# Four modulation groups of the first layer change their stage

## The chip, the core and the metric

The kernel runs on one core of one Trainium2 chip. The metric is the device time of one execution in microseconds (us). The program is one long stream of instructions per engine: TensorE (PE, with its weight loads listed apart as PEld), VectorE (DVE), ScalarE (ACT), GpSimd (POOL) and SyncE (SP), which issues nearly all DMA transfers. In the profile, L247 means line 247 of the kernel.

## The reference, cut to what matters

Two groups of 128 tokens (context and latent) pass through two layers with the same weights. Each layer has a mixer sub-layer and a feed-forward sub-layer, and both are steered by a modulation vector that depends on a conditioning vector only, not on the tokens:

```python
mod = silu(cond) @ w_mod[l] + b_mod[l]            # (2048) x (2048, 12288), for two conds
sh1, sc1, g1, sh2, sc2, g2 = split(mod, 6)
h = rmsnorm(x) * (1 + sc1) + sh1
x = x + g1 * rmsnorm(mixers(h) @ w_out)           # attention, Fourier, RWKV-7 scan
h = rmsnorm(x) * (1 + sc2) + sh2
x = x + g2 * rmsnorm(conv_ffn(h))                 # 2048 -> 2 x 5632 -> 2048
```

Everything is float32. The last piece of a layer's modulation, g2, is used only when the last part of the feed-forward is written out.

## The kernel before

Activations are kept transposed: channels on the 128 partitions, the 256 tokens of both groups along the free dimension. All large weights are streamed once from HBM. A weight block of 256 rows by 512 columns (512 KB) is loaded by `weights_` (L388) into one of the seven buffers of the pool `raw`, cast by ACT to float32r as `hi` (L398), and DVE writes the rest, `raw - hi`, as `lo` (L399). The matmuls then work on the pair: in the mixer's projections three passes per tile (`mm3`, L408 to L410, 256 columns each), in the feed-forward one pass of 512 columns for `hi` (L437) and one of 256 for `lo` (L438).

**Modulation.** The 12288 columns of a layer's modulation are cut into 24 groups of 512 columns: group 4*s+k is quarter k of piece s (sh1, sc1, g1, sh2, sc2, g2), so groups 20 to 23 are g2. `modulation` (L239 on) is a generator that computes one group on TensorE, in five steps. Four steps each load two blocks of 512 KB of `w_mod` (L234) and issue four float32 matmuls on them (L247; eight records in the trace, two for each matmul) into the bank `mb`. The fifth lets DVE transpose the bank (L250, tile `pm`). The closing part, four tiny matmuls (L254, tile `mc`) and one or two small DVE additions (`mod_end`, L304), comes with the call that starts the next group. After the input projection of the first layer the blocks of `w_mod` take their buffers from the same pool of seven as the weights do (`mraw`, `self.early = 0`).

**What sets their place.** A queue `modq` holds the groups that TensorE computes: 24 of layer 0, then 8 to 19 of layer 1. The other 12 of layer 1 are computed on DVE (`modulation_v`, lines L266 to L286, tiles `vraw`, `va`, `vb`) during the two feed-forwards. Each matrix product calls `tick` after each of its weight blocks, and the tick runs as many steps of the queue as a rate has accumulated:

```python
def tick(self, n=1.0):
    self.credit += self.rate * n
    while self.credit >= 1:
        self.credit -= 1
        self.mod_step()
```

`gemm` and `gemm_wide` call `self.tick(0.5)` once per 256 rows of weights. The rate is a constant per stage: `AR` in the outer input projection, `MR[l][0..6]` in the seven stages of the mixer, `QR[l]` in the fourth part of the output projection, `FR[l]` in the feed-forward:

```python
step(0, self.in_proj(l, h, st, ["kv"]))
step(1, ... in_proj ["q"] merged with attention)
step(2, ... in_proj ["xf"])
step(3, self.ticked(self.fourier(st)))
step(4, self.merge(wo(2, ev1), self.heads(l, st, (0, 1)), 16, QM[2]))
step(5, self.merge(wo(0, ev2), self.heads(l, st, (2, 3)), 16, QM[3]))
step(6, wo(1, ev2))
```

`step(n, main)` sets `self.rate = MR[l][n]` and drives the RWKV scan beside `main`. Each of these products has eight ticks of a half, that is 4.0, and the Fourier stage has two whole ones. After them come `wo(3)` with `QR`, the norm, and the feed-forward with `FR`: 11 blocks of up-projection with 16 half ticks each and 11 of down-projection with 8 each, 264 half ticks or 132 ticks. `need` runs steps at once where a group is wanted and not there yet: groups 8 to 11 ahead of `wo(3)`, 12 to 19 in the second `pre_norm`, 20 to 23 ahead of the last down-projection.

Of the kernel before, what the change touches and what calls it, by code (L numbers as in the profile page):

```python
# [33 lines left out]
for _t in (VEC, VEC2):  # L34
# [17 lines left out]
    [[0.8, 0.8, 0.578], [0.88, 0.8, 0.8], [0.96, 0.8, 0.8], [1.0], [1.0, 1.0, 1.0, 1.0], [1.287, 1.3, 1.183, 1.3], [1.45, 1.45, 1.45]],  # L52
]
MR = [
    [1.2, 1.2, 1.2, 2.3, 2.3, 2.185, 4.0],
    [2.4, 2.4, 2.4, 2.4, 2.4, 2.4, 4.5],
]
AR = [
    [2.25, 2.5, 2.5, 0.0],
    [0.0, 0.0, 0.0, 0.0],  # L60
]
QR, FR = [2.0, 1.0], [0.165, 0.4]

VG = [[(1, j) for j in (0, 4, 1, 5, 2, 6, 3, 7)], [(1, j) for j in range(20, 24)]]
VR = [0.58, 0.4]
# [1314 lines left out]
```

## Time and profile before

| | us |
|---|---|
| median of 3 runs | 2700.96 |
| lowest, highest | 2700.59, 2710.13 |
| the profiled execution, its own time | 2702.25 |
| its span in the trace | 2700.5 |

The stages of the profiled execution, by the first matmul of each, are: set-up and outer input projection to 177.3, mixer of layer 0 to 544.8, its `wo(3)` and norm to 607.8, feed-forward of layer 0 to 1396.7, then layer 1: input projection to 1503.6, mixer to 1876.2, `wo(3)` and norm to 1928.3, feed-forward to 2677.2, output to 2700.5. A stretch A:B is given in us from the span's start. Busy time is time with at least one instruction of an engine running; an instruction's record includes its passage through the engine, so consecutive matmuls overlap, and what one costs is read from start to start.

### The profile page before, as it was taken

How to read it: one execution, taken by the hardware profiler on the slowest of the kernel's cores; microseconds unless marked ns; L12 is line 12 of the kernel's file. 1: busy time of each engine (PE TensorE's matmuls, PEld its weight loads, DVE VectorE, ACT ScalarE, POOL GpSimd, SP SyncE). 2: the span in 40 equal slices, each digit the busy share in tenths (PEclk: the TensorE clock that was granted, in tenths of full speed). 3: DMA queues.
4: the chain of work that ended last, by engine and by line, in shares of the span. 5: the costliest groups of instructions: out<-in, count | busy, mean ns of one | idle time of the engine just before them, and what ended most of it. 6: DMA issues, size and time to landing. Idle time of an engine off the chain costs nothing.

```text
span 2700.5 us, 45794 instructions
## 1 busy us (share of the span) xinstructions
PE 2598.5 (96%) x18019; PEld 2141.4 (79%) x18019; DVE 1969.5 (73%) x3316; ACT 1313.4 (49%) x2065; POOL 69.1 (3%) x114
## 2 busy tenths in 40 slices
PE   7999999979999999999989999999799999999998
PEld 4578788748888888888869777778588888888886
DVE  3467857469977898869666768575899669865675
ACT  2256545246554455445434555443555545544553
POOL 1101000000000000000000000000000000000000
PEclk9999999989999999999989999999899999999998
DMA  9965646776777787777655777366377567555552
GB/s 363 382 210 197 218 145 193 253 268 208 252 240 268 250 269 241 250 251 239 204 175 149 238 254 258 125 208 202 99 260 242 188 219 257 188 187 189 186 187 86
DMA packets 316184, 593.93 MB, mean 220 GB/s; under 512 B 22726, under 2 KB 37602, under 8 KB 315968
## 3 DMA queue, kind: packets, MB, share of 16 engines
q1 hardware_dynamic: 314336, 589.54, 65.6%
q8 instruction: 141, 2.31, 0.3%
q0 software_dynamic: 1632, 1.46, 0.2%
q14 instruction: 75, 0.61, 0.1%
HBM read 583.78 MB, written 7.14 MB: 219 GB/s over the span
## 4 chain that ended last, share of the span: by engine, by line
PE 86%; DVE 6%; DMA 3%; ACT 2%; issue 1%; SPq 0%; ACTq 0%; DVEq 0%
PE wm L437 37%; PE wm L438 18%; PE mb L247 5%; PE mm L408 4%; PE mm L409 4%; PE mm L410 4%; PE b L408 2%; PE b L409 2%; PE b L410 2%; PE px L1091 1%; DMA raw<-in_w_in 1%; PE pr L1085 1%; DMA raw<-in_w_out 1%; DVE lo L399 1%; PE vb L286 1%
## 5 line engine op out<-in xcount | busy, mean ns | idle before, releaser
L398 ACT CAST hi<-raw 128x1024 fp32r<-128x1024 f32 (+1 forms) x712 | 735.0, 1033 | 890.6 <-PE wm L437 605.4
L399 DVE TENSOR_TENSOR lo<-raw,hi 128x1024 fp32r<-128x1024 f32 (+1 forms) x712 | 855.9, 1203 | 403.8 <-ACT hi L398 388.6
L437 PE MATMUL wm<-hx,hi 128*128 128x512 f32 x2816 | 990.0, 397 | 10.9 <-DVE hx L591 10.9
L438 PE MATMUL wm<-hx,lo 128*128 128x256 f32 x2816 | 785.2, 279 | 0.0
L437 PEld LDWEIGHTS wm<-hx,hi 128*128 128x128 f32 x2816 | 530.0, 188 | 145.2 <-DVE hx L591 14.3
L438 PEld LDWEIGHTS wm<-hx,lo 128*128 128x128 f32 x2816 | 532.4, 189 | 2.6 <-issue 1.7
L437 PE MATMUL wm<-g,hi 128*128 128x512 f32 x1408 | 496.0, 398 | 0.0
L438 PE MATMUL wm<-g,lo 128*128 128x256 f32 x1408 | 393.6, 280 | 0.0
L437 PEld LDWEIGHTS wm<-g,hi 128*128 128x128 f32 x1408 | 265.2, 188 | 68.7 <-issue 7.1
L438 PEld LDWEIGHTS wm<-g,lo 128*128 128x128 f32 x1408 | 266.3, 189 | 3.2 <-issue 2.9
L280 DVE SCALAR_TENSOR_TENSOR va<-vraw,cst,va 128x512 f32<-128x512 f32 x360 | 256.4, 749 | 0.9 <-DMA vraw<-in_w_mod 0.7
L247 PE MATMUL mb<-raw,cst 128*32 128x512 f32 x1152 | 198.7, 614 | 9.6 <-DVE mod L304 5.1
L408 PE MATMUL mm<-hx,hi 128*128 128x256 f32 x544 | 158.5, 295 | 5.6 <-ACT hx L590 4.1
L409 PE MATMUL mm<-hx,hi 128*128 128x256 f32 x544 | 156.2, 288 | 0.5
L410 PE MATMUL mm<-hx,lo 128*128 128x256 f32 x544 | 155.1, 287 | 0.0
L408 PE MATMUL mm<-mx,hi 128*128 128x256 f32 x512 | 152.7, 299 | 1.8 <-ACT mx L367 1.3
L409 PE MATMUL mm<-mx,hi 128*128 128x256 f32 x512 | 146.7, 287 | 0.2 <-DVE mx L368 0.2
L410 PE MATMUL mm<-mx,lo 128*128 128x256 f32 x512 | 145.2, 287 | 1.5 <-DVE lo L399 1.5
L408 PEld LDWEIGHTS mm<-hx,hi 128*128 128x128 f32 x544 | 104.0, 193 | 34.1 <-issue 16.6
L408 PEld LDWEIGHTS mm<-mx,hi 128*128 128x128 f32 x512 | 98.0, 192 | 26.9 <-issue 21.4
L409 PEld LDWEIGHTS mm<-hx,hi 128*128 128x128 f32 x544 | 104.9, 193 | 5.4 <-issue 4.0
L410 PEld LDWEIGHTS mm<-hx,lo 128*128 128x128 f32 x544 | 104.5, 193 | 4.3 <-issue 3.9
(346 smaller groups left out, 3330.2 us busy)
## 6 DMA issues: line engine op xcount, KB each, us to landing
raw<-in_ffn_w_up SPq DMA_DIRECT2D x352, 512.0 KB, 4.4
raw<-in_w_mod SPq DMA_DIRECT2D x288, 512.0 KB, 5.6
raw<-in_ffn_w_down SPq DMA_DIRECT2D x176, 512.0 KB, 4.3
vraw<-in_w_mod SPq DMA_DIRECT2D x96, 512.0 KB, 5.0
raw<-in_w_in SPq DMA_DIRECT2D x80, 512.0 KB, 5.6
raw<-in_w_out SPq DMA_DIRECT2D x64, 512.0 KB, 5.2
raw<-in_w_uq SPq DMA_DIRECT2D x16, 384.0 KB, 4.0
raw<-in_w_in SPq DMA_DIRECT2D x16, 320.0 KB, 4.2
```

The lines of the kernel that those rows point to most:

```text
L247: nc.tensor.matmul(b[32 * q:32 * q + 32, :], self.cst[:, 4 * kg + q, :], r[:, f, :], start=kg == 0, stop=kg == 3)
L280: nc.vector.scalar_tensor_tensor(a, r[:, f, :], c, a, op0=ALU.mult, op1=ALU.add)
L286: nc.tensor.matmul(b2[:, a, g:g + 1], acc[g][:, 128 * a:128 * a + 128], self.c(C_ONE, 1), start=a == 0 and g == 0, stop=a == 3 and g == 1)
L398: nc.scalar.copy(hi[:, :, 0:w], r)
L399: nc.vector.tensor_tensor(lo[:, :, 0:w], r, hi[:, :, 0:w], op=ALU.subtract)
L408: mm(out, whi, xhi, start=start, stop=False)
L409: mm(out, whi, xlo, start=False, stop=False)
L410: mm(out, wlo, xhi, start=False, stop=stop)
L437: mm(ps[m], hi[:, kk, s], x[:, :, kk, :], start=ki == 0 and k2 == 0 and kk == 0, stop=False)
L438: mm(ps[m][:, 0, :], lo[:, kk, s], x[:, 0, kk, :], start=False, stop=ki == n - 1 and k2 == 1 and kk == 1)
L1085: mm(pr[js, n, :], AP[n // 4, d][ks, n % 4, js], rh[ks, n, :], start=n == 0, stop=n == 7, tile_position=(0, 32 * j))
L1091: mm(px[js, n, :], XT[js, 8 * d + n, :], R[js, n, :], start=n == 0, stop=n == 7, tile_position=(32 * j, 32 * j))
```

## The change

Only rates of layer 0 change: those of the mixer's first three stages and of the two merged output projections go up, and that of the feed-forward goes down. The sequence of steps in the queue and the work of each step stay as they are.

```diff
 MR = [
-    [1.2, 1.2, 1.2, 2.3, 2.3, 2.185, 4.0],
+    [2.2, 2.2, 2.2, 2.3, 3.1, 3.1, 4.0],
     [2.4, 2.4, 2.4, 2.4, 2.4, 2.4, 4.5],
 ]
 AR = [
     [2.25, 2.5, 2.5, 0.0],
     [0.0, 0.0, 0.0, 0.0],
 ]
-QR, FR = [2.0, 1.0], [0.165, 0.4]
+QR, FR = [2.0, 1.0], [0.02, 0.4]
```

## Rows read from the trace of the kernel before

**Rows 1.** The page: span, and part 1, busy us and share.
```profile
span 2700.5 us, 45794 instructions
...
PE 2598.5 (96%) x18019; PEld 2141.4 (79%) x18019; DVE 1969.5 (73%) x3316; ACT 1313.4 (49%) x2065; POOL 69.1 (3%) x114
```

**Rows 2.** Stretches: mixer, feed-forward, each of layers 0 and 1; all engines.
```profile
core 0: us, PE busy (x) PEld busy (x) DVE busy (x) ACT busy (x) POOL busy (x), PEclk, DMA share, GB/s
177.30:544.80 367.50, 357.06 (x3333) 285.64 (x3331) 250.12 (x514) 182.71 (x368) 26.23 (x38) 0.99 0.63 208
...
607.80:1396.70 788.90, 787.20 (x4542) 667.93 (x4543) 652.23 (x978) 391.68 (x526) 0.00 (x0) 0.99 0.72 240
...
1503.60:1876.20 372.60, 357.50 (x3370) 285.19 (x3369) 255.31 (x519) 186.77 (x372) 24.92 (x38) 1.00 0.65 219
...
1928.30:2677.20 748.90, 747.28 (x4310) 650.55 (x4311) 566.35 (x834) 389.78 (x524) 0.00 (x0) 1.00 0.61 199
```

**Rows 3.** The same stretches, line L247 alone: PE busy, PEld busy, clock, DMA.
```profile
177.30:544.80 367.50, 53.45 (x336) 9.01 (x336) 0.99 0.63 208
...
607.80:1396.70 788.90, 18.11 (x136) 2.67 (x136) 0.99 0.72 240
1503.60:1876.20 372.60, 55.65 (x360) 9.77 (x360) 1.00 0.65 219
```

**Rows 4.** The same, line L254 alone: layer 0's mixer and feed-forward.
```profile
177.30:544.80 367.50, 2.71 (x80) 1.71 (x80) 0.99 0.63 208
...
607.80:1396.70 788.90, 0.99 (x32) 0.63 (x32) 0.99 0.72 240
```

**Rows 5.** Timeline of PE around one step in the feed-forward: start, us, what.
```profile
644.75 0.27 PE L438 MATMUL wm<-hx,lo 128*128 128x256 f32 x1
...
648.57 0.28 PE L438 MATMUL wm<-hx,lo 128*128 128x256 f32 x1
648.78 1.07 PE L247 MATMUL mb<-raw,cst 128*32 128x512 f32 x8
649.77 0.50 PE L437 MATMUL wm<-hx,hi 128*128 128x512 f32 x1
...
650.23 0.40 PE L437 MATMUL wm<-hx,hi 128*128 128x512 f32 x1
...
654.83 0.40 PE L437 MATMUL wm<-hx,hi 128*128 128x512 f32 x1
```

**Rows 6.** Timeline of PE around one step in the mixer of layer 0.
```profile
238.84 0.28 PE L410 MATMUL mm<-hx,lo 128*128 128x256 f32 x1
239.05 1.06 PE L247 MATMUL mb<-raw,cst 128*32 128x512 f32 x8
240.05 0.39 PE L408 MATMUL mm<-hx,hi 128*128 128x256 f32 x1
```

**Rows 7.** Groups by line, feed-forward of layer 0, then of layer 1: L286.
```profile
L286 PE MATMUL vb<-const,va 128*128 128x1 f32 x128 | 15.5, 252 | 0.0
...
L286 PE MATMUL vb<-const,va 128*128 128x1 f32 x64 | 7.4, 245 | 0.0
```

**Rows 8.** Two short stretches of layer 0, columns as in the first stretches.
```profile
492.80:499.70 6.90, 6.90 (x40) 4.02 (x37) 0.00 (x0) 1.42 (x3) 0.00 (x0) 0.51 0.69 245
1318.90:1325.70 6.80, 6.80 (x26) 6.03 (x26) 2.87 (x6) 0.31 (x1) 0.00 (x0) 0.50 0.26 84
```

**Rows 9.** Waits in 177.3:544.8: who for whom, total us, times, longest.
```profile
ACT hi L398 <- DMA raw<-in_w_out: 22.0, 5, 7.1
```

**Rows 10.** Waits of SP's queue, 177.3:544.8.
```profile
SPq L234 <- PE mb L247: 89.0, 22, 17.4
SPq L388 <- PE mb L247: 57.6, 18, 7.7
```

**Rows 11.** Waits of SP's queue, 607.8:1396.7.
```profile
SPq L388 <- PE mb L247: 21.7, 16, 3.0
```

**Rows 12.** The page, part 6: loads of `w_mod` for TensorE.
```profile
raw<-in_w_mod SPq DMA_DIRECT2D x288, 512.0 KB, 5.6
```

**Rows 13.** Line L250: shortest, median, longest ns, first and last start.
```profile
L250 DVE STREAM_TRANSPOSE pm<-mb x36: 674/711/719, 25.5 to 1856.1; 128x512 f32<-128x512 f32 x36
```

## The prediction

> **What bounds the kernel now.** I read the page's head first: PE is busy 96% of the span, VectorE 73% [rows 1]. A mean over stages does not say what a step is worth, so I cut the span at the first matmul of each stage and compared the two layers [rows 2]. In the feed-forward of layer 0 PE is busy 787.2 of 788.9 us: it never waits, and anything taken off it there comes off the time. In layer 0's mixer it is busy 357.1 of 367.5 us, so at most 10.4 us are idle: it is nearly the bound there too. Work is therefore moved from one stretch in which TensorE is full to another in which it is almost full, and the question is what one step costs in each.
>
> **How many steps move.** Layer 0's mixer adds up, stage by stage, 3 x 4 x 1.2 + 2 x 2.3 + 4 x 2.3 + 4 x 2.185 + 4 x 4.0 = 52.9 steps; after the change 3 x 4 x 2.2 + 2 x 2.3 + 8 x 3.1 + 4 x 4.0 = 71.8. With the fractions carried along this is 52 steps before and 71 after. The feed-forward's 132 ticks give 22 steps at 0.165 and 3 at 0.02. So 19 steps move: 15 matmul steps, the four transposes of groups 20 to 23, and three of the four closings (that of group 23 comes with the next step, in the feed-forward). What is left of the feed-forward's steps is the beginning of layer 1's group 8, as now; layer 1 starts from the same state of the queue, and nothing in it changes. Groups 12 to 19, which the second norm needs, are ready earlier; groups 20 to 23 are needed much later, so no `need` is forced.
>
> **What the feed-forward gives back.** The rows show 136 records of L247 there, that is 17 steps [rows 3]; one more ran in the gap ahead of it. In the timeline a `lo` matmul starts at 648.57 and the next `hi` at 649.77 with one step between [rows 5]: 1.20 us, where without a step it is 0.11 to 0.12, so a step costs 1.09 us. (17 x 1.09 = 18.5, against 18.1 us of busy time.) Three steps stay, so 14 go: 15.3 us. A closing is 0.99 / 4 = 0.25 us [rows 4]; three make 0.8. The fifteenth step ran in the norm's gap, where PE waits for the norm anyway; I give it 0.5 between nothing and 1.09.
>
> There is a second item, seen only between the rows. From 644.75 to 648.57 there are 11 pairs of `hi` and `lo`, 347 ns each; from 650.23 to 654.83, after the step, 13 pairs of 354 ns [rows 5]. How often the stream is in the slower pace I take from the layers: the feed-forward of layer 0 is 788.9 - 748.9 = 40.0 us longer than layer 1's [rows 2], with the same matmuls. 18.5 us are steps, 1.0 closings, 15.5 - 7.4 = 8.1 the closings of the groups on VectorE [rows 7], 3.4 half of a 6.8 us stretch in which the granted clock was 0.50, 1.2 instead of 2.4 GHz [rows 8]. That leaves 9.0 us, which the slower pace would explain, since 2112 pairs by 7 ns are 14.8 us. With three steps instead of seventeen some of it comes back, between nothing (one early step sets the slow pace and it stays) and all 9.0. The three stand at half ticks 20, 120 and 220 of 264, so most of the stream still lies behind a step; I take 2.5. Sum: 15.3 + 0.8 + 0.5 + 2.5 = 19.1 us less, bounds 16.1 and 26.2.
>
> **What the mixer pays.** In a dense stretch a step costs the same: 238.84 to 240.05 less 0.12, that is 1.09 us [rows 6]. Over the whole stage it is more, because steps are split by other work when the second of their two loads is late: 53.45 / 42 = 1.27 us in layer 0 (two of them at half clock, [rows 8]), 55.65 / 45 = 1.24 in layer 1 [rows 3]. I take 1.24: 15 x 1.24 = 18.6, and three closings of 2.71 / 10 = 0.27 [rows 4], 0.8, in all 19.4. The floor is what the idle time could swallow: 19.4 - 10.4 = 9.0. The ceiling comes from the layers: layer 1's mixer has 45 steps and lasts 372.6 us, layer 0's 42 and 367.5 [rows 2, 3]; 5.1 / 3 = 1.7 us per step gives 26.3. Some waits will be covered by the added work (I take 2 us) and some weights will come later (2 us, see the rival), so 19.4 stands.
>
> **What travels along.** Thirty loads of 512 KB, 15.7 MB [rows 12], enter SP's queue in the mixer. It moves 208 GB/s x 367.5 us = 76 MB now; 92 MB in some 387 us are 238 GB/s, which the feed-forward moves today at 240 without PE idling [rows 2]. So bandwidth hides them; if it did not, 15.7 MB at 240 GB/s would be 65 us, which no row suggests. The four transposes are 4 x 0.71 = 2.8 us of VectorE [rows 13] in a stage where it is busy 250 of 367 us; in the feed-forward it was no bound at 652 of 789. Both I cost at nothing. If VectorE were the cover that is gone in the scan, it would cost the 2.8 us at most.
>
> A rule of the Trainium skill bears here: its page Perfetto Trace Analysis, section Identifying the Most-Contended Engine, says that matmul busy time is a poor measure of TensorE's headroom and that the busy share of weight loads is the better one. By that share the mixer has more room (285.6 / 367.5 = 78%) than the feed-forward (667.9 / 788.9 = 85%), and if the added work took that room first, the mixer would grow by its floor, 9.0 us, and the time would fall by about 10. The layers' comparison above does not bear this out: three steps more, 5.1 us more.
>
> **Sum.** 2702.25 - 19.1 + 19.4 = 2702.6 us for the profiled execution. It stands 1.3 us above the median of the runs, so 2701 us for the median.
>
> **The rivals.** *The mixer swallows the steps.* In layer 0's mixer the scan makes PE wait for VectorE and ScalarE; steps placed in these waits are free. With all 10.4 us used and the feed-forward wholly in the faster pace, 9.0 - 26.2 = -17.2: 2684 us. For it: TensorE's idle time is there, and its steps are independent of the scan. Against it: TensorE takes its instructions in order, and a tick does not know where a wait will be; layer 1's mixer, with more steps in the early stages, still has 15.1 us idle [rows 2]. It decides if the mixer grows by less than about 5 us.
>
> *The seven buffers.* A block of `w_mod` holds a buffer from its load until its step. In the mixer weight loads already wait 57.6 us in 18 waits for such a buffer, 3.2 each and up to 7.7 [rows 10], in the feed-forward 21.7 us in 16, 1.4 each [rows 11]. ScalarE then waited five times for a block of the output projection, 22.0 us, up to 7.1 [rows 9]. Today PE has other work in most of these waits. With rates of 3.1 in the two merged projections two such waits in the open would cost 14.2 us, and a stretch at half clock behind them 3.4 [rows 8]: 2701 + 17.6 = 2719 us. For it: the feed-forward has long matrix products as a cover and the mixer has not. Against it: layer 1's mixer takes 2.4 everywhere and idles no more than 5 us longer. Three uncovered waits of the mean length, or two long ones, decide it. The Trainium skill (Perfetto Trace Analysis, section Optimization Strategy) says that gaps that repeat on the engine that should be full can mean too few buffers; no row shows PE waiting so today.
>
> *The change moves less than it says.* A rate could round away, or `need` could pull steps back. The count above excludes it; the time would be that of before, 2701, and no outcome could be told from the forecast's.
>
> **How the numbers follow.** A difference of 0.5%, 13.5 us, is about what a measurement of this kernel can tell from no change. I give the forecast, an exchange at nearly the same price, 0.80, the third rival included, the swallowing mixer 0.08, the buffers 0.12. The bounds of the two sums give 9.0 - 26.2 = -17 to 26.3 - 16.1 = +10, and a first uncovered wait with half a clock stretch would add some 3 to the top: 2684 to 2715. Cutting the lower tail, where two unlikely ends must meet, leaves 2688 to 2714 with less than 2 in 10 outside. Faster by over 0.5% 0.08, within 0.80, slower 0.12.
>
> **What the profile after would show.** Step count: 24 records of L247 in layer 0's feed-forward instead of 136, and some 456 instead of 336 in the mixer. The feed-forward of layer 0 at about 770 us, the mixer at about 387. If the feed-forward shrinks by 26 the pace was the larger item; if the mixer grows by less than 9 it had room that the idle time does not show; if it grows by over 30, look for ScalarE waiting on loads of the output projection, PE idle above 15 us and more stretches at half clock. Layer 1 should keep its 1280 us to within 3; if it moves, the prediction is wrong in a place that it left out.

## The result, and the profile after

The changed kernel takes 2722.39 us (median of 5 runs, 2718.52 to 2725.47), the kernel before beside it 2704.48 us (5 runs): 1.0063 times as long, 95% interval 1.0046 to 1.0080, that is 12 to 22 us more. The forecast was an exchange at 2701 us with a range of 2688 to 2714 us, so it was wrong: the change is slower, by more than the noise of the runs. Of the 21 us between 2722 and 2701, 18 are the change; the rest is the kernel before itself, whose median was 2700.96 in the three runs that the forecast started from. The profiled execution took 2725.47 us.

The head of the page after, to be held against [rows 1]:

```profile
span 2723.7 us, 45803 instructions
...
PE 2612.1 (96%) x18019; PEld 2151.1 (79%) x18019; DVE 1971.0 (72%) x3316; ACT 1314.4 (48%) x2065; POOL 68.0 (2%) x114
```

The work is the same, and TensorE is busy 13.6 us longer with it in this profile. The heads of the other profiles below read 2598.6 and 2610.2 us before, 2599.3, 2609.5 and 2605.0 after, so most of these 13.6 belong to the one execution. What differs in all of them is TensorE's idle time: 102 to 103 us of the span before, 112 to 116 after. The stretches, cut as in [rows 2], with the gap of the second norm between the first layer's mixer and its feed-forward:

```profile
175.30:575.60 400.30, 385.90 (x3483) 295.37 (x3483) 254.26 (x525) 182.50 (x367) 25.01 (x38) 0.98 0.68 229
575.60:642.50 66.90, 47.55 (x349) 30.88 (x347) 43.00 (x74) 26.16 (x42) 1.30 (x2) 0.86 0.68 236
642.50:1406.90 764.40, 762.72 (x4399) 660.92 (x4400) 647.70 (x966) 392.44 (x526) 0.00 (x0) 1.00 0.69 228
...
1513.90:1898.20 384.30, 366.99 (x3371) 290.99 (x3370) 256.09 (x519) 186.06 (x372) 25.08 (x38) 0.97 0.63 213
...
1949.80:2701.30 751.50, 749.75 (x4310) 651.52 (x4311) 567.41 (x834) 389.46 (x524) 0.00 (x0) 1.00 0.61 198
```

The feed-forward of layer 0 gave back 788.9 - 764.4 = 24.5 us, more than the forecast's 19.1. Its mixer grew from 367.5 to 400.3 us, by 32.8 where 19.4 was said. The gap grew from 63.0 us (544.8 to 607.8 before) to 66.9, and layer 1's mixer, which the change does not name, from 372.6 to 384.3 us. Line L247 by the same stretches, beside [rows 3]:

```profile
175.30:575.60 400.30, 73.36 (x456) 12.52 (x456) 0.98 0.68 229
...
642.50:1406.90 764.40, 3.19 (x24) 0.47 (x24) 1.00 0.69 228
```

456 records in the mixer and 24 in the feed-forward: the steps moved exactly as counted.

**Taking the clock out.** Single profiles of one and the same program differ in how long the granted clock was 0.50. So I multiply each span by its mean granted clock: the length at full speed, as far as TensorE sets the length (a stretch where it does not is shown under *whole_setup*). In three profiles of the kernel before it is 2649.2, 2650.1 and 2650.8 us, in four of the changed kernel 2663.8, 2662.1, 2665.5 and 2664.0 us (spans and clocks in the table behind the experiments). The change costs some 14 us at full speed. By stretch, each length less half of its time at 0.50 (the trace gives these times; a row prints the clock only in hundredths):

| us at full speed | before, 3 profiles | after, 4 profiles | mean difference | forecast |
|---|---|---|---|---|
| mixer, layer 0 | 364.0 to 364.6 | 391.8 to 395.0 | +29.0 | +19.4 |
| gap of its second norm | 55.0 to 56.3 | 57.3 to 57.5 | +1.6 | -0.5 |
| feed-forward, layer 0 | 783.2 to 783.7 | 761.8 to 762.6 | -21.4 | -18.6 |
| layer 1, end to end | 1256.6 to 1257.9 | 1259.0 to 1264.1 | +4.4 | 0 |

The sum is +13.6. Ten of it are what the mixer took above its forecast.

**The rival that looked likelier than the others, the seven buffers, is a small part at most.** The waits of SP's queue and of ScalarE in the mixer after:

```profile
SPq L234 <- PE mb L247: 112.5, 36, 22.7
...
SPq L388 <- PE mb L247: 33.7, 20, 4.1
```

```profile
ACT hi L398 <- DMA raw<-in_w_in: 21.6, 7, 9.7
ACT hi L398 <- DMA raw<-in_w_out: 21.4, 7, 9.6
```

and, of the same waits before, the one that neither [rows 9] nor [rows 10] has:

```profile
ACT hi L398 <- DMA raw<-in_w_in: 1.9, 1, 1.9
```

Weight loads wait less for a block's buffer than before (33.7 us against 57.6, [rows 10]), and ScalarE waits for the output projection as long as before (21.4 against 22.0, [rows 9]). One wait did grow: ScalarE's for blocks of the input projections, from 1.9 to 21.6 us (10.7 to 19.8 in the other three profiles after). Little of it reaches TensorE: the recorded waits of its projection matmuls for a cast block (L408 and L410) add up to 1.1 us before and 2.4 after, those of their weight loads to 1.5 and 5.9. The larger item stands in TensorE's own order. The timeline of PE at the beginning of the mixer after:

```profile
177.30 0.28 PE L410 MATMUL mm<-hx,lo 128*128 128x256 f32 x1
177.50 1.04 PE L247 MATMUL mb<-raw,cst 128*32 128x512 f32 x2
178.48 1.12 PE L840 MATMUL b<-sq,const 128*128 128x512 f32 x2
179.44 0.60 PE L853 MATMUL b<-const,v 128*128 128x128 f32 x4
179.97 1.06 PE L247 MATMUL mb<-raw,cst 128*32 128x512 f32 x6
180.96 0.39 PE L408 MATMUL mm<-hx,hi 128*128 128x256 f32 x1
```

A step is four matmuls, 8 records. Here one of the four runs alone, 177.50 to 178.48, and after a piece of the scan the other three, 179.97 to 180.96. Each piece takes 0.98 or 0.99 us; a whole step takes 1.00 us from its start to the next instruction ([rows 6]). The four write four strips of 32 partitions and run side by side; a part of them costs as much as all four. I cut all of L247 in the first mixer into such pieces (runs of records with no other matmul between; time from the first one's start to the next other matmul's, half-clock pieces left out of the means):

| records in a piece | before, second profile: pieces, us each | after, second profile |
|---|---|---|
| 1 to 3 | 9: five of 0.98 to 1.00 us, four of 0.05 (another matmul starts beside them) | 10, of 0.98 to 1.98 us, mean 1.08 (with waits) |
| 4 | 3, 0.98 | 4, 0.98 |
| 5 to 7 | 9, 0.95 to 1.62 | 8, mean 1.21 (with waits) |
| 8 | 20, 1.00 | 19, 1.00 |
| 10 to 16 | 6, 1.84 or 1.85 | 15, 1.84 to 1.87 |
| all pieces, time at full speed | 47, 48.6 us | 56, 71.2 us |

So 15 more steps take 22.6 us, 1.51 each. The rest of the mixer's growth is in other lines, among them the projections (tile `mm`: 152.6 to 153.0 us in the profiles before, 154.3 to 157.2 after, by the same count). By stages, at full speed, the mixer's first three, which take ten of the 15 steps, grew by 18.4 us, its last three by 10.6.

### The profile page after: what moved, and what is told of

The parts are those of the page before. It is cut to its first block, busy times and chain, and to the rows that moved or that the text cites. A ratio compares the mean times of both kernels' runs of the same rounds, so it can differ in the third digit from the quotient of the medians.

```text
span 2723.7 us, 45803 instructions
## 1 busy us (share of the span) xinstructions
PE 2612.1 (96%) x18019; PEld 2151.1 (79%) x18019; DVE 1971.0 (72%) x3316; ACT 1314.4 (48%) x2065; POOL 68.0 (2%) x114
## 5 line engine op out<-in xcount | busy, mean ns | idle before, releaser
L437 PEld LDWEIGHTS wm<-hx,hi 128*128 128x128 f32 x2816 | 530.0, 188 | 140.7 <-DVE hx L591 13.8
L438 PE MATMUL wm<-g,lo 128*128 128x256 f32 x1408 | 391.8, 279 | 0.0
L247 PE MATMUL mb<-raw,cst 128*32 128x512 f32 x1152 | 202.0, 609 | 6.6 <-DMA raw<-in_w_mod 3.8
L408 PE MATMUL mm<-hx,hi 128*128 128x256 f32 x544 | 160.1, 298 | 5.5 <-ACT hx L590 4.1
L410 PE MATMUL mm<-hx,lo 128*128 128x256 f32 x544 | 156.0, 289 | 1.8 <-DVE lo L399 1.8
L408 PE MATMUL mm<-mx,hi 128*128 128x256 f32 x512 | 152.2, 299 | 1.2 <-ACT mx L367 1.1
L410 PE MATMUL mm<-mx,lo 128*128 128x256 f32 x512 | 146.0, 288 | 3.6 <-DVE lo L399 3.5
L408 PEld LDWEIGHTS mm<-hx,hi 128*128 128x128 f32 x544 | 105.3, 195 | 34.6 <-issue 15.0
L408 PEld LDWEIGHTS mm<-mx,hi 128*128 128x128 f32 x512 | 97.7, 191 | 30.6 <-issue 25.8
L410 PEld LDWEIGHTS mm<-hx,lo 128*128 128x128 f32 x544 | 105.9, 195 | 7.4 <-issue 5.1
```

Of the source, the lines that this page charges most:

```text
L247: nc.tensor.matmul(b[32 * q:32 * q + 32, :], self.cst[:, 4 * kg + q, :], r[:, f, :], start=kg == 0, stop=kg == 3)
L408: mm(out, whi, xhi, start=start, stop=False)
L410: mm(out, wlo, xhi, start=False, stop=stop)
L437: mm(ps[m], hi[:, kk, s], x[:, :, kk, :], start=ki == 0 and k2 == 0 and kk == 0, stop=False)
L438: mm(ps[m][:, 0, :], lo[:, kk, s], x[:, 0, kk, :], start=False, stop=ki == n - 1 and k2 == 1 and kk == 1)
```

## Experiments

Theories: *splits* (steps laid among the scan and the projections are taken apart, and each part costs a whole one), *loads and buffers* (15.7 MB more arrive in the mixer), *place* (one of the rates is to blame), *order* (the build arranges layer 1 anew, although its rates are the same), *chance* (the loss belongs to one execution). *Price* in the expectations is a moved step that costs some 2 us in the mixer, for whatever reason. Times are medians; each ratio is to the kernel before, on the same chip.

**The changed kernel once more** (no edit).

> The changed kernel once more, nothing altered. Three theories of its 0.6%. Price: a modulation step costs about 2 us in the first layer's mixer instead of 1.24; order: the instructions of the second layer stand in another order, although its rates did not change, and that costs some 14 us there; chance: the second layer's 14 us (1280.5 to 1294.4 us from the end of the first feed-forward to the end of the second) were this one execution's, with 17 us at half clock in its mixer where the kernel before had none. Price and order: 18 to 23 us above the kernel before, second layer again at 1292 to 1296 us. Chance: the second layer within 3 us of 1280 in this profile, and 5 to 12 us above the kernel before.

2725.6 us, 1.0072 (1.0053 to 1.0091). The loss stands. Its profile shows layer 1's mixer at 376.8 us instead of 384.3, with the granted clock at 1.00 instead of 0.97:

```profile
1512.90:1889.70 376.80, 359.49 (x3369) 286.07 (x3369) 256.12 (x519) 186.28 (x372) 25.04 (x38) 1.00 0.65 217
```

So most of what the first profile showed in layer 1 was the clock of that execution.

**Only the early stages' rates, and only the merged projections'.**

```
early:  MR[0] = [2.2, 2.2, 2.2, 2.3, 2.3, 2.185, 4.0]   FR[0] = 0.072
late:   MR[0] = [1.2, 1.2, 1.2, 2.3, 3.1, 3.1, 4.0]     FR[0] = 0.11
```

> Only the first three rates go up (2.2), and the feed-forward keeps 10 of its 22 steps: 12 steps move into the projections kv, q and xf, none into the merged output projections. The instructions of the second layer stand in the order of the changed kernel. Price with the projections as the place: first layer's mixer 20 us or more above its 367.5 us, feed-forward about 12 us below 788.9. Order: second layer 1292 to 1296 us, as in the changed kernel, and 15 us or more above the kernel before in all. Chance: second layer near 1280 us, 3 to 8 us above the kernel before.

> Only the two merged output projections go to 3.1, and the feed-forward keeps 15 steps: 7 steps move. The order in the second layer is a third one. Price with the output projections as the place (buffers held, weights late): mixer 15 us or more above 367.5 us. Price with the projections as the place: mixer plus 7 to 10 us, feed-forward minus 8, no difference in all from the first layer. Order: the second layer anywhere between 1275 and 1296 us, and the time follows it.

Early: 2725.49 us, 1.0077 (1.0060 to 1.0093). Late: 2715.68 us, 1.0046 (1.0029 to 1.0063). L247 in their mixers, early first:

```profile
175.80:574.40 398.60, 65.92 (x408) 10.79 (x408) 0.97 0.65 215
```

```profile
177.30:558.60 381.30, 56.38 (x376) 9.37 (x376) 0.99 0.65 215
```

At full speed the mixer is 388.3 us with 51 steps and 376.2 with 47: +24 for 9 and +12 for 5, no cheaper per step than all 15 together. No single rate is to blame. By the count of the table above, only 4.8 of the 12 us in *late* are L247's own, and 12.4 of the 24 in *early*; the rest stands in the projections (3.5 and 8.2) and other lines. Splits alone explain neither run.

**Nothing moved, one neutral number changed.**

```
-QR, FR = [2.0, 1.0], [0.165, 0.4]      (the kernel before)
+QR, FR = [2.0, 1.0], [0.16, 0.4]
```

> The kernel before with a feed-forward rate of 0.16 instead of 0.165: no step changes its stage, 22 steps stay in the feed-forward, some one or two ticks later. The first layer's mixer is instruction for instruction that of before; the second layer's order changes in 74 places on TensorE. Price: first layer as before within 3 us, no change in all (within 4 us). Order: the second layer moves by 5 us or more one way or the other and the time with it. Chance: differences only in half-clock stretches that another profile would not repeat.

2711.94 us, 1.0027 (1.0016 to 1.0039): 7 us for a number that moves no step out of its stage. TensorE's order in the first mixer is that of before, and that stretch is 364.3 us at full speed, as before; in layer 1 the order differs in some 70 places. There the time went:

```profile
1504.20:1887.70 383.50, 364.33 (x3371) 289.29 (x3370) 255.75 (x519) 185.71 (x372) 28.24 (x38) 0.98 0.64 213
```

1264.0 us for layer 1 at full speed, against 1256.6 to 1257.9. The changed kernel has some 40 such places there. That nothing in layer 1 changes was true of the source, not of the program built from it. Six profiles with the changed kernel's order there give 1258 to 1267 us, four with that of before 1257 to 1259: some 4 us, with ends that touch.

**The last moved groups without their loads.** Groups 20 to 23 of layer 0 multiply a tile that is already on the chip; their blocks of `w_mod` are not loaded.

```
-                r = self.mod_raw(w, i, 512 * kg + 256 * e)
+                r = (self.later.rearrange("p (c n) -> p c n", c=2) if l == 0 and i >= 20
+                     else self.mod_raw(w, i, 512 * kg + 256 * e))
```

> The changed kernel without the loads of the four moved groups: groups 20 to 23 of layer 0 multiply a tile that is resident anyway, so their 30 loads in the mixer and 2 beyond it are left out and g2 of layer 0 is wrong; every TensorE, VectorE and ScalarE instruction stays. So far the first layer's mixer is 392 to 395 us long with half-clock time taken out at half, against 364 before, 1.9 us per moved matmul step. Theory loads (the moved blocks hold buffers and make the weights late): the mixer falls to about 383, the 19 us of TensorE time alone, and the kernel by 8 to 12 us against the changed one. Theory place (what costs is that steps on TensorE stand between the scan's and the products' instructions, with or without loads): the mixer stays at 390 or above and the time within 4 us of the changed kernel.

2714.16 us, 1.0049 (1.0031 to 1.0066). Mixer and gap:

```profile
179.40:573.80 394.40, 379.58 (x3484) 291.68 (x3482) 257.07 (x529) 185.06 (x369) 24.95 (x38) 0.99 0.64 213
573.80:634.20 60.40, 47.12 (x351) 30.12 (x347) 39.95 (x71) 24.04 (x40) 1.30 (x2) 0.84 0.36 112
```

The run tests less than its expectation says. The steps without loads are the last ten of the mixer and six in the gap behind it (529.2 to 606.9 us), and 20 loads are missing in the mixer, 12 in the gap. The rates of the first three stages draw earlier groups forward, and these keep their loads. The mixer is still 391.0 us at full speed, so the volume of the last groups' loads is not its price; whether the earlier loads in the first stages cost something is not shown. The steps are still split (11 pieces of 2 records, 9 of 6), nearly all of them steps with loads; of those without, two are. What the run gains is in the gap: 51.0 us at full speed instead of 57.4, with 112 GB/s there instead of 236.

**One more buffer for the blocks** (`RAW` 7 to 8; for want of room `VRAW` 3 to 2).

> The changed kernel with eight buffers instead of seven for weights and modulation blocks, and two instead of three for VectorE's own modulation blocks to make room. Theory loads by buffers held: the mixer of layer 0 at 385 us or less (half-clock time taken out at half) instead of 392 to 395. Theory place: 390 to 396. The second layer's order changes too, so only the first layer's stages are read.

2723.49 us, 1.0078 (1.0066 to 1.0090). Not faster. The mixer was 387.5 us at full speed, between the two forecasts, with 6 pieces of 2 records instead of 10; of the 5.8 us less than in the changed kernel 4.6 are L247's own, which leaves little for the buffers. The feed-forward took 3.5 us more.

**The other direction**: steps of layer 1's groups from its mixer into layer 0's feed-forward.

```
-    [2.4, 2.4, 2.4, 2.4, 2.4, 2.4, 4.5],        (MR[1] of the kernel before)
+    [1.6, 1.6, 1.6, 1.6, 1.6, 1.6, 4.5],
-QR, FR = [2.0, 1.0], [0.165, 0.4]
+QR, FR = [2.0, 1.0], [0.3, 0.4]
```

> The opposite direction: the first layer's rates as before, but 18 more steps (groups 8 to 11 of layer 1) come into its feed-forward (rate 0.3), out of the second layer's mixer, whose rates fall to 1.6. If a step costs 1.09 to 1.5 us in the feed-forward and 1.5 to 2 in a mixer: first feed-forward at 788.9 + 15 x 1.1 to 1.5 = 805 to 812 us, second mixer 371 - 15 x 1.5 to 2 = 341 to 349 us with half-clock time taken out, in all 0 to 13 us faster than the kernel before. If the price is the same in both, no change; if the order of the second layer decides, anything within 8 us.

2709.56 us, 1.0029 (1.0014 to 1.0044): slower, where 0 to 13 us less was expected.

```profile
604.40:1410.10 805.70, 804.00 (x4679) 669.61 (x4680) 656.86 (x990) 391.72 (x526) 0.00 (x0) 1.00 0.77 252
1517.00:1883.80 366.80, 349.85 (x3226) 286.51 (x3225) 251.28 (x507) 186.88 (x372) 23.95 (x38) 0.98 0.55 182
```

At full speed the feed-forward pays 18 us, and layer 1's mixer, with 14 steps fewer (248 records instead of 360), gives back 11, that is 0.8 each. A mixer step is worth 0.8 us where it is taken from 45 in layer 1 and costs 1.9 where it is added to 42 in layer 0, so the price is no constant. How it depends on the count is not shown: layer 1's order is rebuilt here too, which alone was worth 7 us in *shift*.

**A second profile of the kernel before** (no edit).

> The kernel before once more, for a second profile of it. Both theories: first mixer 367 us again within 4 us, second layer from 1277 to 1290 us. Theory chance: its half-clock stretches in the two mixers differ by several us from the 6.8 and 3.4 us of the first profile. Theory order: the second mixer, with half-clock time taken out at half, again at 371 us within 1 us.

2703.23 us, span 2701.4, mixers of 364.6 and 380.5 us. Layer 1's mixer was 372.6 in the first profile; at full speed it is 371.0 there and 372.0 here.

**Whole steps.** Both loads first, then the four matmuls, those of the later load ahead, so that the build can lay all four side by side. Put into the changed kernel (*whole*) and into the kernel before (*whole_before*):

```
-            for e in range(2):
-                r = self.mod_raw(w, i, 512 * kg + 256 * e)
-                for f in range(2):
-                    q = 2 * e + f
-                    nc.tensor.matmul(b[32 * q:32 * q + 32, :], self.cst[:, 4 * kg + q, :], r[:, f, :], ...)
+            r = []
+            for e in range(2):
+                r.append(self.mod_raw(w, i, 512 * kg + 256 * e))
+            for q in (2, 3, 1, 0):
+                nc.tensor.matmul(b[32 * q:32 * q + 32, :], self.cst[:, 4 * kg + q, :], r[q // 2][:, q % 2, :], ...)
```

> The changed kernel, with one difference: both loads of a modulation step are issued first and then its four matmuls, the two that need the later load ahead, so that the four stand side by side in TensorE's order. Theory, splitting: a piece of one to four matmuls takes about 1.0 us, because the four fill four 32-column groups of the array together, so the mixer's 57 steps cost 71.5 us in 56 pieces where whole they would cost some 56 to 58. Then layer 0's mixer without its half-clock loss falls from 392 to 395 us to 377 to 382, its L247 pieces of 2 and 6 records are gone, and the run is 2706 to 2714 us. Rival, waiting: TensorE then stands waiting for the later of the two loads, and the mixer stays at 388 us or more although the pieces are whole, with PE waits on DMA at L247 of 8 us or more; time 2720 to 2730 us.

> The kernel before with the same difference as in the run above and no other. Splitting: layer 0's 42 mixer steps cost 48.6 us in 47 pieces; whole they cost about 42, so the mixer falls from 364 to 357 to 360 us and the time by 0 to 10 us. The pair then tells the price of a moved step without splits: mixer of the run above less mixer of this one, over 15, should be 1.1 to 1.4 us, as forecast, instead of 1.9. Rival, waiting: the difference stays at 1.8 us or more per step, so that the price lies in the place and not in the splits.

Whole: 2703.27 us, 0.9993 (0.9979 to 1.0006). Whole_before: 2694.74 us, 0.9962 (0.9944 to 0.9980). The first mixer is 382.9 and 363.6 us at full speed: 19.3 us for the 15 steps and three closings, the forecast's 19.4. By the medians the change still costs 8.5 us with whole steps in both kernels, so the splits are about half of its 18. *Whole* came out below its forecast of 2706 to 2714 us, for it gains ahead of the mixer too, and its mixer just above its 377 to 382. No piece shorter than 8 records is left in that mixer (32 of 8, 11 of 16, one of 24). L247 ahead of the mixer and in it, first in *whole*, then in *whole_before*:

```profile
0.00:160.20 160.20, 39.05 (x264) 5.92 (x264) 0.93 1.00 361
160.20:551.60 391.40, 58.04 (x456) 10.31 (x456) 0.98 0.70 234
```

```profile
0.00:160.10 160.10, 38.01 (x264) 5.71 (x264) 0.94 1.00 360
160.10:528.80 368.70, 44.23 (x336) 7.99 (x336) 0.99 0.64 206
```

(58.04 - 44.23) / 15 = 0.92 us per added step; a step is 58.04 / 57 = 1.02 and 44.23 / 42 = 1.05 us in the mean, where it was 1.27 to 1.29. So the 19.4 came out partly by chance: the steps' own busy time is 13.8 us of it, not 18.6, and the rest is waiting and other lines. And the kernel before got nothing for whole steps in its own mixer, 363.6 us against 364.0 to 364.6:

```profile
160.10:528.80 368.70, 351.78 (x3331) 287.61 (x3330) 247.63 (x513) 181.94 (x367) 26.45 (x38) 0.99 0.64 206
```

TensorE's busy time there fell from 357.06 to 351.78 us, and its idle time rose from 10.4 to 16.9. With 42 steps, what whole steps save came back as idle time; with 57, most of it came off the length (next experiment). What *whole_before* gains lies ahead of the mixer, where the modulation's first groups were split as well.

**Which part of it does what.** *whole_later* is the changed kernel with whole steps from the first mixer on (setup as it was); *whole_setup* the kernel before with whole steps in setup alone.

```
+            r, last = [], not self.early        (whole_setup: self.early)
...
+            for q in (2, 3, 1, 0) if last else range(4):
```

> The changed kernel with the four matmuls of a step kept together from layer 0's mixer on, and its setup as it was. If the extra price of the moved steps is the splitting, layer 0's mixer without its half-clock loss is 380 to 385 us as in the run with whole steps everywhere (383.0), not 392 to 395, the stretch ahead of the mixer stays at 175 to 177 us, and the time is 2709 to 2718 us, some 10 below the changed kernel. If the mixer was shorter there only because more of its work had been done ahead of it, the mixer is back at 390 us or more and the time at 2722 to 2728 us.

> The kernel before with the four matmuls of a step kept together ahead of layer 0's mixer alone; TensorE's order in the feed-forward of layer 0 and in the whole of layer 1 is that of before, and most of the first mixer's. If the gain of the kernel before with whole steps everywhere (2694.7 us) lies in the stretch ahead of the mixer, that stretch is about 160 us instead of 177 here too and the time is 2688 to 2696 us. If that stretch only gets ahead on work that the mixer then lacks, the mixer grows by as much and the time stays at 2701 to 2706 us.

Whole_later: 2715.03 us, 1.0044 (1.0026 to 1.0061), by the ratios 5 to 8 us below the changed kernel (1.0063 and 1.0072), with intervals that overlap; the mixer tells more. All engines in it, L247 in it, and the same place as in the timeline above:

```profile
178.20:569.90 391.70, 372.23 (x3484) 292.74 (x3483) 253.66 (x526) 182.25 (x367) 25.22 (x38) 0.98 0.70 233
```

```profile
178.20:569.90 391.70, 58.83 (x456) 10.30 (x456) 0.98 0.70 233
```

```profile
180.22 0.28 PE L410 MATMUL mm<-hx,lo 128*128 128x256 f32 x1
180.43 1.06 PE L247 MATMUL mb<-raw,cst 128*32 128x512 f32 x8
181.43 1.13 PE L840 MATMUL b<-sq,const 128*128 128x512 f32 x2
```

The mixer is 383.2 us at full speed, and 382.0 in the second profile below: some 10 less than the changed kernel's 391.8 to 395.0. Of these, 3 lie in the first three stages and 7 in the last three; the ten steps added to the first three cost 15 us even whole. The step that took 177.50 to 178.48 and 179.97 to 180.96 takes 180.43 to 181.43. Whole_setup: 2694.5 us, 0.9964 (0.9953 to 0.9976), with layer 1 in the order of before. Its stretch ahead of the mixer is 161.4 us, and L247 costs 40.24 us there for 264 records, against 60.98 before:

```profile
0.00:161.40 161.40, 40.24 (x264) 6.05 (x264) 0.92 0.99 357
```

```profile
0.00:177.30 177.30, 60.98 (x264) 8.91 (x264) 0.99 0.91 326
```

The second line is the kernel before. That is the whole gain of *whole_before*, and this version is faster than the kernel before and the changed one.

In this stretch the product of length and clock misleads. Four steps of setup, first in *whole_setup* wholly at 0.50, then in the second profile of the kernel before (there partly in halves) at 1.00:

```profile
27.80:40.00 12.20, 7.74 (x32) 0.83 (x32) 2.81 (x3) 1.04 (x1) 0.00 (x0) 0.50 1.05 387
```

```profile
26.50:38.40 11.90, 7.93 (x32) 1.15 (x32) 3.83 (x5) 1.33 (x2) 0.00 (x0) 1.00 1.05 386
```

TensorE waits for blocks of `w_mod` in both, and at half the clock they took 0.3 us more, not twice as long. The products of the three versions with whole steps in setup are therefore too low as lengths at full speed; for these the spans and times count.

**Is the rest the clock?** Unchanged kernels, one profile each: before, after twice, whole_later.

> The kernel before, unchanged, for a third profile. If the time at half clock belongs to the program, its mean granted clock is 0.981 again and the span 2700 to 2702 us; if it belongs to the execution, the clock is anywhere from 0.976 to 0.982 and the span follows it by 2.7 us for each 0.001.

> The changed kernel, unchanged, for a third profile. Span times mean clock was 2663.8 and 2662.1 us in the two profiles at hand, with clocks of 0.978 and 0.981. Both theories: that product is 2660 to 2666 us again. Clock of the program: 0.976 to 0.979. Clock of the execution: anywhere from 0.976 to 0.982.

> The same kernel once more. If the change brings time at half clock with it, at least two of the four profiles of the changed kernel lie below 0.979 and all of the kernel before at 0.980 or more; if not, the two sets overlap.

> The changed kernel with whole steps from the mixer on, for a second profile. Span times clock was 2647.9 us, as in the kernel before (2649.2), at a clock of 0.976. If its remaining 10 us come from the clock that this program gets, the clock is 0.975 to 0.978 again; if that was the one execution, it is 0.980 to 0.982 and the span 2696 to 2704 us, and the 10 us of the timed runs stay unexplained.

| profile | span us | mean granted clock | product us |
|---|---|---|---|
| before, three | 2700.5, 2701.4, 2713.2 | 0.981, 0.981, 0.977 | 2649.2, 2650.1, 2650.8 |
| after, four | 2723.7, 2713.6, 2722.7, 2721.2 | 0.978, 0.981, 0.979, 0.979 | 2663.8, 2662.1, 2665.5, 2664.0 |
| shift | 2712.7 | 0.980 | 2658.4 |
| whole_later, two | 2713.0, 2721.6 | 0.976, 0.974 | 2647.9, 2650.8 |
| whole, whole_before | 2697.2, 2684.2 | 0.973, 0.979 | 2624.4, 2627.8 |
| whole_setup | 2692.2 | 0.975 | 2624.9 |

(A clock printed to 0.001 leaves the product uncertain by 1.4 us.) The clocks of before and after overlap, so single profiles cannot tell what the clock has in the loss. All executions whose span and clock are on record can: 75 of the kernel before have a mean clock of 0.9807 and a mean product of 2651.1 us, 13 of the changed kernel 0.9787 and 2663.5, eight of *whole_later* 0.9758 and 2649.7. So some 12.7 us of the change's loss are length at full speed, and some 5.5 a lower clock. *Whole_later* is at full speed as long as the kernel before, and its loss of 10 us is the clock. Why these programs are granted less is not settled: TensorE stands idle in the first mixer for 10.4 to 10.7 us in the kernel before, 14.4 to 17.0 in the changed one and 19.3 to 19.5 in *whole_later*, but that this is the reason was not tried.

## Why the prediction was wrong

**Count of steps: right.** 24 and 456 records, as said.

**The feed-forward's 19.1: right in kind, low in size.** 24.5 us by the two first profiles, 21.4 at full speed; the rest of the 24.5 is half-clock time that the feed-forward of before had in its first profile. Steps and closings are 16.1 of it as costed. That leaves some 5 for the slower pace of the stream and the group left to the gap, where the forecast took 2.5 + 0.5.

**The mixer's 19.4: the step that failed.** Its text was "I take 1.24: 15 x 1.24 = 18.6", and the ceiling of 26.3 came from comparing two layers. It cost 29.0, above the ceiling. The parts that the text knew of, "steps are split by other work", were priced at the mean of a mixer in which making the steps whole gains nothing (*whole_before*); with the added steps it gains 10 us. That the splits are 10 of the 29 us is shown by *whole_later*, twice: it removes them and nothing that the change moves. With whole steps in both kernels the price is 19.3, near the forecast partly by chance, as said there. The mechanism of the other lines' share (*early*, *late*, and the 15 us of the first three stages with whole steps) stays open. A rival is left for it: ScalarE gets blocks of the input projections later, and no run took out the loads that stand ahead of them.

The reason given there for the splits, "when the second of their two loads is late", does not fit most of them: one matmul of a load stands apart from the other of the same load in the timeline above, 2 records and 6, and *noload* has two steps split without loads. The pieces are the same in all four profiles of the changed kernel, so they are laid out when the program is built; by what rule stays open.

**That nothing in layer 1 changes: wrong**, in the place that the text had named as its test. Its order is rebuilt; about 4 us, and *shift* shows 7 for a neutral number. **The gap: wrong by about 2 us**: the last two steps of group 22 and all of group 23 now stand there, and 0.5 of gain had been written down.

**Loads and transposes at nothing: not refuted in the mixer**, where DMA moved 229 GB/s against the 238 of the estimate, and where *noload*, with 20 loads fewer, is 391.0 us against a mean of 393.3; the earlier loads of the first stages, and the transposes, were not taken out. In the gap the run without 12 loads is 6 us shorter, so there they cost something.

**The rivals.** *The mixer swallows the steps* was excluded by its own point, a growth under 5 us. The rule weighed there, the Trainium skill's page Perfetto Trace Analysis, section Identifying the Most-Contended Engine, judges TensorE's headroom by MFU (the share of its peak arithmetic) and by the busy share of the weight loads. By the second, 78%, the mixer had room; this case disagrees: the share after is 295.37 / 400.30 = 74%, and the mixer grew by 29 us at full speed. *The seven buffers* came near in time, 2719, but by the wrong way: the weight loads' waits for buffers fell, the kernel with an eighth buffer was no faster, and only the blocks of the input projections came later.

The sum with the measured terms: 29.0 + 1.6 - 21.4 + 4.4 = +13.6 at full speed, 13.9 at a clock of 0.98, inside the measured 12 to 22. With the 5.5 us of the lower clock it is 19.4, against 17.9 by the medians. The prediction's sum has no term for a clock that changes.

## What to carry to other kernels

Before you move small work into a stage, look in the timeline at how that work is laid there, not at its mean: instructions that are cheap only side by side are paid once for every piece that the program's order makes of them. Whether the pieces cost time has to be tried: here making the steps whole gained nothing in the mixer with 42 steps and 10 us in the same mixer with 57. Give such a group one common last condition (here the matmuls of the later load first); ahead of the first mixer that alone was worth 10 us. When a builder lays out the order, time a neutral change of one number first: here it was worth 7 us, where the change under study cost 18.

## What the hardware showed that was not expected

- Two, four, six or eight records of the 32-column matmul take 0.98, 0.98, 0.99 and 1.00 us where no wait is among them (mixer of layer 0, *again*). In setup, 35 pieces of 4 records took 1.03 us each (*before*), and 20 of 8 records 1.08 (*whole_before*).
- In its profiles the same program gets mean clocks from 0.977 to 0.981 (before) and 0.978 to 0.981 (after); span times clock repeats within 1.6 us and 3.4 us. This product tells 14 us from nothing where the spans (2713.2 before, 2713.6 after) do not. It fails where TensorE waits for DMA: four steps of setup took 12.20 us at 0.50 and 11.90 at 1.00.
- The price of a step is no constant: 0.8 us each for 14 taken out of layer 1's mixer with 45, 1.9 each for 15 added to layer 0's with 42.
